# A fourth row buffer, fetches three units ahead, and weight sums spread evenly, in an encoder layer on one core

## The chip, the cores and the metric

The kernel runs on one core of a Trainium2 chip. The metric is the device time of one execution in microseconds (us), lower is better; the median over runs is compared.

## The reference

One layer of a streaming encoder for two groups of tokens, 2048 of a prompt and 8 x 16 of samples, width 1024. Cut to its frame:

```python
h   = rms_norm(x, norm_g[0]);  z = h @ w_in          # 3592 columns
att = band_attention(...)                            # 8 heads x 64, own chunk of 64 and 8 before
mem = mlstm_sequence(...)                            # 4 heads x 128, matrix memory
x   = x + rms_norm(concat(att, mem) @ w_out, norm_g[1])
h   = rms_norm(x, norm_g[2])
u   = h @ w_up                                       # 1024 -> 2 * 2816
y   = b_conv + sum(ext[:, j:j + S] * w_conv[j] for j in range(3))   # causal, depthwise
gate, up = split(y, 2)
ffn = (gelu(gate) * up) @ w_down                     # 2816 -> 1024
x   = x + rms_norm(ffn, norm_g[3])
```

All is float32. The change concerns the last matrix product, `w_down`, alone.

## The kernel before, in words

**Precision.** Every float32 operand `r` of a matrix product is split into a high part (`h`, a cast on ACT, L1259) and the rest (`l = r - h`, on DVE, L1260); `mm3` (L95 to L97) makes three matmuls of each product: high by high, high by low, low by high. So every activation row and every weight block passes a cast and a subtraction before TensorE can use it.

**Stages.** After the projections, attention and memory come 17 token tiles of 128 rows in three blocks (`FBLOCKS`: 6, 6 and 5 tiles). For each block the kernel runs an up stage and then a down stage.

The up stage has 22 units `f` of 128 columns. It computes `u` as a two-by-two block product with seven products in place of eight (P1 to P7), applies the convolution (`conv`: one ACT and two DVE instructions on a row of 768), GELU and the product of the halves, and stores the activation row `g` to DRAM: to `gd` (blocks 0 and 2, called plain), or with six further combinations of the token halves to `gsd` (block 1).

The down stage reads these rows back. In plain blocks it goes twice (`dh` = 0, 1: the two halves of the output's 1024 columns) over 22 steps `k`, one row of `gd` each, with weights in six chunks of four `k` (the last of two); the row is needed again in the second half and fetched again. In block 1 it runs 42 units `q`: seven products (D1 to D7) of six units, each unit a row of `gsd` with two blocks of weights. Four of the seven products need sums or differences of weight quarters. These are made in block 0, beside its down stage, and kept in DRAM (`wtd`).

**Buffers.** Two pools matter. `row` (tag "yq") has three buffers of 128 x 1024 and holds the convolution's rows (`y`, `g`), fetched activation rows (`gr`, `gq`), squares of the norm and evacuated halves. `quad` (tag "q") has eleven buffers of 128 x 512 and holds raw weights (`wu`, `wdr`, `wt`), pieces of the next block's transposed rows, evacuated halves, and the first few activation rows of a down stage, fetched as two halves (`early`), while the convolution still needs the rows. The split parts of an activation row lie in `w3` (four buffers: two rows in flight), those of weights in `wh` and `wl` (two each: the present chunk and the next).

**Fetches.** `fetch(dh, k)` and `fetch_unit(q)` load a row. At the end of the up stage the first ones go early into quads: 0 to 4 in plain blocks, 0 to 3 in block 1. From then on, step k calls the fetch of row k + 2 (L1732, L1733; unit q of q + 2, L1645, L1646). All these DMAs are issued on SP's queue, which takes them one after the other: an instruction there that waits for its data or for a free buffer holds those behind it.

**Sums.** `load_down` (L1324) loads the weights of a chunk. In block 0 every second chunk also loads the other column half of its (up to) two pairs of k into `wt`, and puts four sums a pair, each with its store, into the list `sums`. Each step k calls `step_sums(3)` (L1346), which takes three of them: a DVE operation in place, and its store on SP right behind it.

**Order.** Instructions are written in a program order, but the framework orders each engine's stream itself by a simulated timeline; it also inserts the waits. `tc.keep_in_program_order` ties one instruction behind the one written before it on the same engine, so that it isn't moved ahead of it.

**Beside the down stage** run `ahead` units, one step of them for every k or q: the norm and transposition of the next block's rows (`h2_units`) and the finish of the block before (`later`: loads `f` and `x`, an update on DVE and POOL, the store of the output).

Of the kernel before, what the change touches and what calls it, by code (L numbers as in the profile page):

```python
# [10 lines left out]
F32 = mybir.dt.float32  # L11
F32R = mybir.dt.float32r
AF = mybir.ActivationFunctionType
ALU = mybir.AluOpType
# [3 lines left out]
P = 128  # L18
D = 1024
# [9 lines left out]
NF = 22  # L29
# [15 lines left out]
def hymba_step(ctx: ExitStack, tc: tile.TileContext, I: dict, O: dict):  # L45
    nc = tc.nc
# [69 lines left out]
    wtd = [dt_([P, 2048], f"wtd{i}") for i in range(NF // 2)]  # L116
# [920 lines left out]
    ffn = SimpleNamespace(B=[None] * 7, p4=None)  # L1037
# [11 lines left out]
    def quad(name):  # L1049
        return ffn.p3.tile([P, 512], F32, tag="q", name=name, bufs=11)  # L1050

    def row(name):
        return ffn.p3.tile([P, D], F32, tag="yq", name=name, bufs=3)

    def new_B(i, b):
        pool = ffn.p3 if i < EARLY_B else ffn.p4
# [138 lines left out]
    for n_, (half, gi) in enumerate(seq):  # L1195
        wh, wl, _ = pend
# [5 lines left out]
        i = int(g[2])  # L1202
# [116 lines left out]
    def block_of(src, i, q):  # L1319
        return src[i][:, q * 512:(q + 1) * 512]  # L1320

    sums = deque()

    def load_down(dh, c, keep_sums):  # L1324

        ks = range(4 * c, 4 * c + (4 if c < 5 else 2))
        at = lambda k, h: ((0, 1), (3, 2))[k % 2][h]
        raws_ = []
        w = load_w([block_of(I["w_down"], k // 2, at(k, dh)) for k in ks], f"{dh}_{c}", raws_)
        if keep_sums and c % 2 == dh:  # L1330
            for x, k in enumerate(ks):
                if k % 2:
                    continue
                t = [None] * 4
                for e in range(2):
                    t[at(k + e, dh)] = raws_[x + e]
                    r = t[at(k + e, 1 - dh)] = quad(f"wt{k + e}")
                    nc.sync.dma_start(r, block_of(I["w_down"], k // 2, at(k + e, 1 - dh)))
                for o, x_, y_, op in ((2, 2, 1, ALU.subtract), (1, 1, 0, ALU.subtract), (0, 2, 0, ALU.add),
                                      (3, 3, 0, ALU.subtract)):  # L1340
                    sums.append((t, o, x_, y_, op, wtd[k // 2][:, KEPT_AT[o] * 512:KEPT_AT[o] * 512 + 512]))
        return w

    KEPT_AT = (2, 0, 1, 3)

    def step_sums(count):  # L1346
        for _ in range(min(count, len(sums))):
            t, o, x_, y_, op, dst = sums.popleft()
            nc.vector.tensor_tensor(t[o], t[x_], t[y_], op=op)
            nc.sync.dma_start(dst, t[o])  # L1350

    D1, D6, D2, D7, D5, D4, D3 = range(7)
    W_RAW, W_SUM = 0, 1
# [88 lines left out]
    for b, tiles in enumerate(FBLOCKS):  # L1442
# [100 lines left out]
        for f in range(NF):  # L1543
            w = pend.pop(0)
# [5 lines left out]
            a, d_, ec = ps_mm(f"ua{nm}"), ps_sm(f"ub{nm}"), ps_big(f"uec{nm}")  # L1550
            e, c = ec[:, 0:512], ec[:, 512:1024]
# [10 lines left out]
            w = pend.pop(0)  # L1562
            ahead_of(2 * f + 3)
            if f == NF - 1 and plain:
                split_g(0, 0, w3_tile)
                split_g(0, 1, w3_tile)
                for k in range(2, 5):
                    fetch(0, k, True)
            elif f == NF - 1:
                split_unit(0)  # L1570
                split_unit(1)
                for q in range(2, 4):
                    fetch_unit(q, True)
# [53 lines left out]
        if not plain:  # L1627
# [4 lines left out]
            for q in range(42):  # L1632
# [9 lines left out]
                        pend = [load_up(b + 1, 0, 0, quads[0])]  # L1642
                if q not in parts:
                    split_unit(q)
                if q >= 2:  # L1645
                    fetch_unit(q + 2)  # L1646
                gh, gl = parts.pop(q)
                for k in range(2 if u < 5 else 1):
                    at = u % 2 * 1024 + k * 512
# [33 lines left out]
        for dh in range(2):  # L1683
# [9 lines left out]
            for c in range(6):  # L1693
# [48 lines left out]
            for j in order:  # L1742
# [5 lines left out]
                else:  # L1748
# [7 lines left out]
        step_sums(len(sums))  # L1756
        if not last:
            while ahead.step():
                pass
# [96 lines left out]
```

## Time and profile before

| | before |
|---|---|
| median of 3 runs | 2805.16 us (2804.77 to 2808.17) |
| profiled execution | 2804.53 us, its span 2802.8 us |
| PE busy | 2717.6 us, 97% of the span |
| DVE busy | 1936.8 us, 69% |
| ACT busy | 1422.5 us, 51% |
| POOL busy | 450.3 us, 16% |
| moved by DMA | 516.36 MB, mean 184 GB/s |

Times inside the trace count from the start of the span. PE is TensorE's matmuls, PEld its weight loads, which overlap with them; a busy PE is not a PE at its peak, since matmuls are pipelined. PEclk is the granted share of TensorE's clock. SPq is SP's queue of DMA issues; "<-" in a row of a timeline leads from what is written to what is read, and in brackets to what ended the idle time before the row. L1259 and so on are lines of the kernel; `split` has one pair of lines for weights and activations, so the tile's name tells them apart: `gh`, `gl` are parts of activation rows, `wdh`, `wdl` of the weights.

### The profile page before, as it was taken

How to read it: one execution, taken by the hardware profiler on the slowest of the kernel's cores; microseconds unless marked ns; L12 is line 12 of the kernel's file. 1: busy time of each engine (PE TensorE's matmuls, PEld its weight loads, DVE VectorE, ACT ScalarE, POOL GpSimd, SP SyncE). 2: the span in 40 equal slices, each digit the busy share in tenths (PEclk: the TensorE clock that was granted, in tenths of full speed). 3: DMA queues.
4: the chain of work that ended last, by engine and by line, in shares of the span. 5: the costliest groups of instructions: out<-in, count | busy, mean ns of one | idle time of the engine just before them, and what ended most of it. 6: DMA issues, size and time to landing. Idle time of an engine off the chain costs nothing.

```text
span 2802.8 us, 47259 instructions
## 1 busy us (share of the span) xinstructions
PE 2717.6 (97%) x16488; PEld 2543.9 (91%) x16488; DVE 1936.8 (69%) x3563; ACT 1422.5 (51%) x2872; POOL 450.3 (16%) x876
## 2 busy tenths in 40 slices
PE   8999999999999999999999999999999899999898
PEld 7899999998899998878999987799999688999887
DVE  5344455656456668666989987658888876888755
ACT  4345555544356666543454555445454665555433
POOL 1000010212000003244212210011111221222211
PEclk9999999999999999999999999999999999999999
DMA  5544355557455565356545467855555896555586
GB/s 187 153 125 128 111 173 156 171 158 218 156 159 147 149 182 168 97 191 215 189 164 173 161 218 248 296 171 172 177 168 172 267 322 222 180 170 180 192 283 202
DMA packets 334462, 516.36 MB, mean 184 GB/s; under 512 B 57138, under 2 KB 162830, under 8 KB 334094
## 3 DMA queue, kind: packets, MB, share of 16 engines
q1 hardware_dynamic: 295630, 479.49, 53.3%
q10 hardware_dynamic: 38592, 33.83, 3.6%
q8 instruction: 130, 2.13, 0.3%
q14 instruction: 110, 0.90, 0.1%
HBM read 371.61 MB, written 144.72 MB: 184 GB/s over the span
## 4 chain that ended last, share of the span: by engine, by line
PE 50%; DVE 5%; DMA 4%; issue 1%; ACT 1%; POOL 1%; SPq 0%; DVEq 0%; ACTq 0%; POOLq 0%
PE uec L95 5%; PE uec L96 5%; PE uec L97 5%; PE dn L95 3%; PE dn L97 3%; PE dn L96 3%; PE ua L97 3%; PE ua L95 3%; PE ua L96 3%; PE dnm L95 2%; PE dnm L97 2%; PE wo L95 2%; PE dnm L96 2%; PE wo L97 2%; PE wo L96 2%; PE ub L96 1%
## 5 line engine op out<-in xcount | busy, mean ns | idle before, releaser
L95 PE MATMUL uec<-B,wuh 128*128 128x384 f32 (+1 forms) x720 | 235.7, 328 | 6.4 <-DVE uu L1578 4.9
L96 PE MATMUL uec<-B,wuh 128*128 128x384 f32 (+1 forms) x720 | 235.2, 327 | 0.0
L97 PE MATMUL uec<-B,wul 128*128 128x384 f32 (+1 forms) x720 | 233.5, 327 | 0.0
L1259 ACT CAST wuh<-wu 128x512 fp32r<-128x512 f32 x255 | 141.6, 617 | 96.0 <-PE uec L96 89.9
L95 PE MATMUL dn<-wdh,gh 128*128 128x512 f32 x444 | 176.3, 397 | 6.8 <-ACT gh L1259 4.3
L96 PE MATMUL dn<-wdl,gh 128*128 128x512 f32 x444 | 176.7, 398 | 0.0
L1260 DVE TENSOR_TENSOR wul<-wu,wuh 128x512 fp32r<-128x512 f32 x255 | 164.8, 683 | 3.1 <-DMA x2d<-mx 3.1
L97 PE MATMUL dn<-wdh,gl 128*128 128x512 f32 x444 | 166.5, 400 | 0.0
L395 DVE CUSTOM_DVE_ANT_0 tmp<-s,nb 128x640 f32<-128x640 f32 (+4 forms) x128 | 94.4, 738 | 95.3 <-PE s L385 93.4
L95 PE MATMUL vo<-wi_h,hT 128*128 128x256 f32 x544 | 155.9, 287 | 0.6 <-DVE mt L201 0.6
L97 PE MATMUL vo<-wi_h,hT 128*128 128x256 f32 x544 | 156.3, 287 | 0.0
L96 PE MATMUL vo<-wi_l,hT 128*128 128x256 f32 x544 | 155.5, 286 | 0.0
L95 PEld LDWEIGHTS uec<-B,wuh 128*128 128x128 f32 x720 | 135.0, 188 | 10.0 <-DVE uu L1578 6.8
L95 PE MATMUL qk<-hT,wi_h 128*128 128x384 f32 (+1 forms) x384 | 130.4, 340 | 5.9 <-ACT qk_st L226 5.2
L96 PEld LDWEIGHTS uec<-B,wuh 128*128 128x128 f32 x720 | 135.2, 188 | 0.1
L97 PEld LDWEIGHTS uec<-B,wul 128*128 128x128 f32 x720 | 135.0, 188 | 0.0
L408 DVE TENSOR_TENSOR ptl<-pt,pth 128x640 fp32r<-128x640 f32 (+4 forms) x128 | 93.7, 738 | 57.7 <-ACT pth L407 56.7
L1260 DVE TENSOR_TENSOR gl<-gr,gh 128x768 fp32r<-128x768 f32 (+3 forms) x92 | 75.7, 830 | 82.6 <-ACT gh L1259 82.6
L1259 ACT CAST gh<-gr 128x768 fp32r<-128x768 f32 (+3 forms) x92 | 65.0, 719 | 131.5 <-PE dn L96 100.5
L396 ACT ACTIVATE tmp<-tmp,mn 128x640 f32<-128x640 f32 (+4 forms) x128 | 97.6, 762 | 64.5 <-DVE mn L395 61.8
L1260 DVE TENSOR_TENSOR wdl<-wdr,wdh 128x512 fp32r<-128x512 f32 x165 | 107.8, 696 | 31.8 <-ACT wdh L1259 31.8
L96 PE MATMUL qk<-hT,wi_h 128*128 128x384 f32 (+1 forms) x384 | 129.0, 336 | 0.0
(440 smaller groups left out, 9080.1 us busy)
## 6 DMA issues: line engine op xcount, KB each, us to landing
wu<-in_w_up SPq DMA_DIRECT2D x220, 256.0 KB, 3.9
wu<-wsd SPq DMA_DIRECT2D x176, 256.0 KB, 3.7
wdr<-in_w_down SPq DMA_DIRECT2D x121, 256.0 KB, 5.3
wi_raw<-in_w_in SPq DMA_DIRECT2D x52, 512.0 KB, 4.1
wsd<-ws SPq DMA_DIRECT2D x88, 256.0 KB, 3.2
gr<-gd SPq DMA_DIRECT2D x39, 384.0 KB, 5.7
kraw<-kTd SPq DMA_DIRECT2D x112, 128.0 KB, 3.4
gr<-gd SPq DMA_DIRECT2D x39, 320.0 KB, 4.1
```

Of the source, the lines that this page charges most:

```text
L95: nc.tensor.matmul(out, ah, bh, start=start, stop=False, skip_group_check=onto)
L96: nc.tensor.matmul(out, ah, bl, start=False, stop=False, skip_group_check=onto)
L97: nc.tensor.matmul(out, al, bh, start=False, stop=stop, skip_group_check=onto)
L395: nc.vector.tensor_tensor_reduce(o_, s_, b_, 1.0, 3e38, ALU.add, ALU.min, accum_out=mn)
L396: nc.scalar.activation(tmp[:, :n], tmp[:, :n], AF.Exp, bias=mn, scale=-1.0, accum_out=rsum[:, i % 4, hh:hh + 1])
L408: nc.vector.tensor_tensor(s.ptl[:, sl, qc], ptv, s.pth[:, sl, qc], op=ALU.subtract)
L1259: nc.scalar.copy(h, r)
L1260: nc.vector.tensor_tensor(l, r, h, op=ALU.subtract)
```

## The change

It does four things. The pool `row` gets a fourth buffer. Fetches in the down stages are called for k + 3 and q + 3 in place of k + 2 and q + 2 (in block 1 unit 2 now goes into a row at once instead of two quads). Each chunk of weights of block 0 makes the sums of one pair of k (the eleven pairs are spread over the first eleven of its twelve chunks) in place of up to two pairs in every second chunk. And the sums are timed by a counter of steps: two in the second step after the load was called, two in the third, their stores two steps after each; both are tied to the program order.

```diff
     def row(name):
-        return ffn.p3.tile([P, D], F32, tag="yq", name=name, bufs=3)
+        return ffn.p3.tile([P, D], F32, tag="yq", name=name, bufs=4)
...
-    sums = deque()
+    later_on = []
+    at_step = [0]
...
         w = load_w([block_of(I["w_down"], k // 2, at(k, dh)) for k in ks], f"{dh}_{c}", raws_)
-        if keep_sums and c % 2 == dh:
-            for x, k in enumerate(ks):
-                if k % 2:
-                    continue
-                t = [None] * 4
-                for e in range(2):
-                    t[at(k + e, dh)] = raws_[x + e]
-                    r = t[at(k + e, 1 - dh)] = quad(f"wt{k + e}")
-                    nc.sync.dma_start(r, block_of(I["w_down"], k // 2, at(k + e, 1 - dh)))
-                for o, x_, y_, op in (...):
-                    sums.append((t, o, x_, y_, op, wtd[k // 2][:, ...]))
+        i = 2 * c + (dh if c < 5 else 0)
+        if not keep_sums or (c == 5 and dh):
+            return w
+        t = [None] * 4
+        for k in (2 * i, 2 * i + 1):
+            t[at(k, dh)] = raws_[k - 4 * c]
+            r = t[at(k, 1 - dh)] = quad(f"wt{k}")
+            nc.sync.dma_start(r, block_of(I["w_down"], i, at(k, 1 - dh)))
+
+        def combine(o, x, y, op):
+            tc.keep_in_program_order(nc.vector.tensor_tensor(t[o], t[x], t[y], op=op))
+
+        def store(o, to):
+            tc.keep_in_program_order(nc.sync.dma_start(block_of(wtd, i, to), t[o]))
+
+        for n_, (o, x, y, op, to) in enumerate(...):
+            due = at_step[0] + 2 + n_ // 2
+            later_on.append((due, lambda a=(o, x, y, op): combine(*a)))
+            later_on.append((due + 2, lambda a=(o, to): store(*a)))
         return w
...
-    def step_sums(count):
-        for _ in range(min(count, len(sums))):
-            t, o, x_, y_, op, dst = sums.popleft()
-            nc.vector.tensor_tensor(t[o], t[x_], t[y_], op=op)
-            nc.sync.dma_start(dst, t[o])
+    def step_sums():
+        for x in [x for x in later_on if x[0] <= at_step[0]]:
+            later_on.remove(x)
+            x[1]()
+        at_step[0] += 1
...
-                for q in range(2, 4):
-                    fetch_unit(q, True)
+                fetch_unit(2)
+                fetch_unit(3, True)
...
-                if q >= 2:
-                    fetch_unit(q + 2)
+                if q >= 1:
+                    fetch_unit(q + 3)
...
-                        fetch(dh, k + 2)
+                        fetch(dh, k + 3)
...
-                    if dh == 1 or k >= 3:
-                        fetch(dh + (k + 2) // NF, (k + 2) % NF)
+                    if dh == 1 or k >= 2:
+                        fetch(dh + (k + 3) // NF, (k + 3) % NF)
...
-                    step_sums(3)
+                    step_sums()
```

More of the change, by code (lines that the diff above doesn't have):

```diff
@@ L1329, in load_down @@
         w = load_w([block_of(I["w_down"], k // 2, at(k, dh)) for k in ks], f"{dh}_{c}", raws_)
-        if keep_sums and c % 2 == dh:
-            for x, k in enumerate(ks):
-                if k % 2:
-                    continue
-                t = [None] * 4
-                for e in range(2):
-                    t[at(k + e, dh)] = raws_[x + e]
-                    r = t[at(k + e, 1 - dh)] = quad(f"wt{k + e}")
[L1338 to L1341, printed above, removed]
-        return w
-    KEPT_AT = (2, 0, 1, 3)
-    def step_sums(count):
-        for _ in range(min(count, len(sums))):
-            t, o, x_, y_, op, dst = sums.popleft()
-            nc.vector.tensor_tensor(t[o], t[x_], t[y_], op=op)
-            nc.sync.dma_start(dst, t[o])
+        i = 2 * c + (dh if c < 5 else 0)
[10 more added lines that the diff above has]
+            tc.keep_in_program_order(nc.sync.dma_start(block_of(wtd, i, to), t[o]))
+        for n_, (o, x, y, op, to) in enumerate(((2, 2, 1, ALU.subtract, 1), (1, 1, 0, ALU.subtract, 0),
+                                                (0, 2, 0, ALU.add, 2), (3, 3, 0, ALU.subtract, 3))):
+            due = at_step[0] + 2 + n_ // 2
+            later_on.append((due, lambda a=(o, x, y, op): combine(*a)))
+            later_on.append((due + 2, lambda a=(o, to): store(*a)))
+        return w
+    def step_sums():
[3 more added lines that the diff above has]
+        at_step[0] += 1
     D1, D6, D2, D7, D5, D4, D3 = range(7)
@@ L1755, in hymba_step @@
                     unfinished.append((tiles[j], rs))
-        step_sums(len(sums))
+        while later_on:
+            step_sums()
         if not last:
```

## The prediction

> **What bounds the kernel now.** I first cut the span into its stages by the view of busy time by windows: all before the FFN, then up and down projection of the three token blocks in turn.
>
> ```profile
> core 0: us, PE busy (x) PEld busy (x) DVE busy (x) ACT busy (x) POOL busy (x), PEclk, DMA share, GB/s
> 1322.00:1651.00 329.00, 320.99 (x1824) 316.71 (x1822) 301.58 (x457) 165.97 (x266) 70.45 (x87) 1.00 0.53 178
> 1651.00:1850.00 199.00, 190.02 (x838) 155.04 (x839) 132.67 (x189) 93.91 (x155) 10.87 (x24) 0.98 0.76 257
> 2166.00:2357.00 191.00, 180.59 (x799) 147.11 (x798) 147.60 (x212) 111.59 (x201) 33.76 (x42) 0.96 0.81 275
> 2638.00:2803.00 165.00, 150.93 (x636) 120.93 (x636) 90.58 (x124) 59.85 (x107) 31.86 (x34) 0.97 0.71 243
> ```
>
> The three down stages (lines 2 to 4) have PE idle for 9 to 14 us each and a granted clock under 1.00; elsewhere TensorE hardly stops. TensorE is the bound, and what a change can win is TensorE's gaps. The chain that ended last shows the steady pace: in block 0 the pair "dnm L97 x2" comes back once per step k.
>
> ```profile
> 1779.26 0.47 PE dnm L97 x2
> ...
> 1783.41 0.47 PE dnm L97 x2
> ...
> 1787.55 0.47 PE dnm L97 x2
> ```
>
> So a step is 4.15 us (1783.41 - 1779.26), and with the data there it is TensorE alone. The timeline of PE has the gaps; the bracket is the idle time before the row, and its releaser.
>
> ```profile
> 1652.18 0.50 PE L95 MATMUL dnm<-wdh,gh 128*128 128x512 f32 x1 [1.80 <-ACT wdh L1259]
> ...
> 1667.15 0.50 PE L95 MATMUL dnm<-wdh,gh 128*128 128x512 f32 x1 [1.22 <-ACT gh L1259]
> ...
> 1683.94 0.80 PE L95 MATMUL dnm<-wdh,gh 128*128 128x512 f32 x1 [3.58 <-ACT gh L1259]
> ...
> 1773.00 0.50 PE L95 MATMUL dnm<-wdh,gh 128*128 128x512 f32 x1 [2.28 <-ACT gh L1259]
> ...
> 2200.18 0.80 PE L95 MATMUL dn<-wdh,gh 128*128 128x512 f32 x1 [4.29 <-ACT gh L1259]
> ...
> 2241.23 1.11 PE L1089 MATMUL h2T_pt<-ident,x2r 128*128 128x128 f32 x4 [3.97 <-ACT b L1106]
> ...
> 2652.93 0.50 PE L95 MATMUL dnm<-wdh,gh 128*128 128x512 f32 x1 [1.23 <-ACT gh L1259]
> 2660.27 0.80 PE L95 MATMUL dnm<-wdh,gh 128*128 128x512 f32 x1 [3.35 <-ACT gh L1259]
> ```
>
> Nearly all wait for "gh", the split of an activation row; and nearly all stand in the first steps of a down stage, where the row buffers change hands from the convolution to the fetches. The four longest are followed by slow matmuls (0.80 and 1.11 us long). The windows behind them:
>
> ```profile
> 1683.90:1689.60 5.70, 5.66 (x17) 4.78 (x18) 5.70 (x9) 1.56 (x3) 0.00 (x0) 0.50 0.83 284
> 2200.20:2205.00 4.80, 4.80 (x13) 3.85 (x14) 3.88 (x4) 2.59 (x5) 1.59 (x3) 0.50 0.81 245
> 2241.20:2245.90 4.70, 4.67 (x13) 3.89 (x14) 3.97 (x7) 2.53 (x5) 0.94 (x1) 0.50 0.99 349
> 2660.30:2665.80 5.50, 5.50 (x13) 4.34 (x14) 3.88 (x5) 0.72 (x1) 3.08 (x2) 0.50 1.05 397
> ```
>
> PEclk is 0.50 in all four: half of each window is lost too, 2.85, 2.40, 2.35 and 2.75 us. With its clock the stall at 1684 costs 3.58 + 2.85 = 6.4, that at 2200 6.7, at 2241 6.3, at 2660 6.1 us; the 2.28 us of 1773 cost no clock (its row has the usual 0.50). The Trainium skill's page "TensorE: Matmul & The Clock Gate", section "Part 1: The HAM clock gate (the "warmup" mystery)", says that an idle window of about 3.4 us halves the clock and a busy one of about 3.4 us restores it. By that an estimate for 1684 would be 3.58 + 1.7 = 5.3; the trace has longer cold stretches, and the row decides.
>
> **The change, part by part.** The simulated scheduler of the framework orders each engine, so I price what comes late, not positions.
>
> *Sums, block 0.* The number of operations stays: eleven pairs, each with two extra loads, four subtractions or additions and four stores. Before, two pairs of every second chunk were summed at three a step; now one pair of every chunk, two sums a step, each store two steps behind its sum and tied behind the SP instruction before it. What this is worth is seen on SP, DVE and ACT ahead of the stall of 1684:
>
> ```profile
> 1671.28 1.59 SPq L1338 DMA_DIRECT2D wt<-in_w_down  x2
> 1673.20 0.33 SPq L1590 DMA_DIRECT2D gd<-g  x1
> 1677.97 0.33 SPq L1350 DMA_DIRECT2D wtd<-wt  x1
> 1678.39 0.38 SPq L1503 DMA_DIRECT2D gr<-gd  x1
> ...
> 1677.25 0.69 DVE L1349 TENSOR_TENSOR wt<-wt,wt 128x512 f32<-128x512 f32 x1 [3.31 <-DMA wt<-in_w_down]
> ...
> 1683.05 0.83 ACT L1259 CAST gh<-gr 128x768 fp32r<-128x768 f32 x1 [1.42 <-DMA gr<-gd]
> ```
>
> SP issued nothing from 1673.53 to 1677.97: the store of a sum stood at its head, the sum waited for its second operand, and the fetch of row 5 stood behind the store. It went out at 1678.39, landed at 1683.05, and TensorE waited. With the store two steps (8.3 us) later, and the fetch called one step (4.15 us) earlier, the row lands at about 1673.6 + 4.7 = 1678.3, before step 4 ends (1683.94 - 3.58 = 1680.4). Gain between 0 (another load takes the store's place at SP's head) and 6.4; I take 5.5, since the rows name the store as cause and, with the cast of 0.83 us, the lead is 1680.4 - 1678.3 - 0.8 = 1.3 us.
>
> *The start of block 0.* Eight sums run in the first steps, first and last:
>
> ```profile
> 1644.02 0.69 DVE L1349 TENSOR_TENSOR wt<-wt,wt 128x512 f32<-128x512 f32 x1 [1.85 <-DMA wt<-in_w_down]
> ...
> 1660.43 0.68 DVE L1349 TENSOR_TENSOR wdr<-wdr,wdr 128x512 f32<-128x512 f32 x1
> ...
> 1664.00:1680.00 16.00, 14.78 (x66) 11.69 (x65) 11.80 (x18) 11.11 (x20) 0.96 (x3) 1.00 0.94 326
> ```
>
> That is 8 x 0.68 = 5.4 us of DVE and 1.85 of waiting, while TensorE waits 1.80 and 1.22 us. They leave this place; but the step counter is 0 when both of the first two chunks are loaded, so eight sums fall due in steps 2 and 3. The third row shows DVE with 16 - 11.80 = 4.2 us free there, so at worst 5.4 - 4.2 = 1.2 comes back. Ends: -1.2 to +3.0; I take +1.5, half the gaps, because the convolution of the last unit holds DVE there as well.
>
> *What the sums add.* A pair now holds four of the eleven quarter-row buffers ("q") from its load to its landed stores, some six steps instead of about three, so the next chunk finds seven for its six loads, and the pieces of the next block's transposed rows want the same buffers. The second half of the stage shows no gap at all with the old bursts, so I cost it at nothing; what it costs without that cover is the second rival. Tying adds no wait of its own: what is queued behind a tied store on SP is the next fetch, and its row is needed three steps on.
>
> *Fourth row buffer and three units ahead, block 1.* In the old trace the first fetch into a row buffer (unit 4), and the split that it holds up, are
>
> ```profile
> 2195.48 1.03 SPq L1527 DMA_DIRECT2D gq<-gsd  x2
> ...
> 2199.30 0.83 ACT L1259 CAST gh<-gq 128x768 fp32r<-128x768 f32 x1
> ...
> 2206.00:2246.00 40.00, 34.68 (x152) 27.54 (x151) 34.62 (x46) 23.77 (x42) 11.43 (x10) 0.91 0.92 320
> ```
>
> It waited for the convolution's last row product and landed under TensorE's gap. Now unit 2 takes a row early and frees it when it is split, and unit 4 can go then, a step or more earlier. That removes up to 6.7 us at 2200. But just behind it, 2206 to 2246 (third row), the DMA engines are busy 0.92 of the time, and the stall of 2241 stands there, where no row is the releaser. Reaching that stretch 6.7 us earlier asks the same bytes of it in less time. So I take half, 3.3; ends 0 and 6.7 + 6.3 = 13.0. The fetch of unit 2 in one transfer instead of two saves one issue on SP, which has gaps: nothing.
>
> *Block 2.* Here the first row fetch stands behind the store of the last activation:
>
> ```profile
> 2648.48 0.32 SPq L1590 DMA_DIRECT2D gd<-g  x1
> 2648.85 0.42 SPq L1503 DMA_DIRECT2D gr<-gd  x1
> ...
> 2658.41 0.62 ACT L1259 CAST wdh<-wdr 128x512 fp32r<-128x512 f32 x1 [0.23 <-DMA wdr<-in_w_down]
> 2659.49 0.72 ACT L1259 CAST gh<-gr 128x640 fp32r<-128x640 f32 x1 [0.47 <-DMA gr<-gd]
> ```
>
> A fourth buffer lets it go before that product is made. The 1.23 us at 2652.93 should go; at 2660 the split also stood behind weight casts on ACT that waited for their own transfer, so of 6.1 I take 1.8. Sum 3.0; ends 0 and 7.3.
>
> *Up stages and the stage before the FFN.* The convolution's rows get the fourth buffer too. The first row of the stage windows has DVE at 301.58 of 329 us, and no DVE work goes away: nothing, ends -3 and +3.
>
> Sum: 5.5 + 1.5 + 3.3 + 3.0 = 13.3 us. The profiled execution took 2804.53 us around a span of 2802.8, 0.6 under the median of 2805.16. So 2804.5 - 13.3 = 2791.2, and on the scale of the medians 2792.
>
> **The rivals.**
> 1. *The transfers are the limit, or the fetch is held by something else.* For it: DMA share 0.94 at 1664 to 1680 and 0.92 at 2206 to 2246, and other waits stand on SP. Then each stall moves a few steps on. Against it: 397 GB/s in the last clock window, so 320 is no ceiling. The page "DMA: Bandwidth & Descriptors" of the Trainium skill, section "Specifications", gives about 358 GB/s of HBM per core; the 397 here is above that. Gains remain below 3 us: 2803.
> 2. *The other side: weight loads starve for quarter-row buffers.* Place: the edges between chunks in block 0 and the change of halves near 1773, where the four held buffers, the six loads and two evacuated halves come together, twelve on eleven. A late weight chunk costs a wait like 1684's, 6.4 us. There are eleven edges. The 6.3 us of blocks 1 and 2 stay; it gets slower than before from the first late edge if block 0 gains nothing, measurably (over 5.6 us) from the second: 2 x 6.4 - 6.3 = +6.5; with three late, +12.9 and 2818. Against it: a chunk is needed four steps, 16.6 us, after its load is called, and the page's section on DMA issues has its landing at 5.3.
>
> ```profile
> wdr<-in_w_down SPq DMA_DIRECT2D x121, 256.0 KB, 5.3
> ```
>
> 3. *Everything goes:* 6.4 + 3.0 + 2.3 + 13.0 + 7.3 = 32.0, the whole of the quoted gaps; with 27 of it the time is 2778. For it: an earlier fetch helps every start alike.
>
> **How the numbers follow.** Forecast 0.65 (its own range 2781 to 2801), rival 1 0.16, rival 2 0.09, rival 3 0.10. A difference under 0.2% (5.6 us) is about what a measurement of this kernel can't tell from none. Of the forecast 0.03 lies inside that band, so faster is 0.62 + 0.10 = 0.72, same 0.19, slower 0.09. The range 2778 to 2808 takes in rival 1 and leaves half of rival 3 and rival 2 out, some 0.15.
>
> **What would show it.** Right: in block 0 a row fetch goes out on SP between 1670 and 1675 and the gap of 3.58 with its half clock is gone; no sum on DVE before the third step; stores never head SP with an unfinished sum; the gap of 4.29 in block 1 is under 1.5, the 1.23 in block 2 gone; the down stages' PEclk nearer 1.00. Wrong: new gaps with "wdh" as releaser at chunk edges of block 0 (rival 2), or the same gaps a few steps on with DMA releasers (rival 1). The forecast fails most easily in block 1, if the gap at 2241 grows by what 2200 loses.

## The result, and the profile after

The changed kernel takes 2790.07 us (median of six runs, 2784.68 to 2792.67) against 2804.89 us (2800.39 to 2808.17): a ratio of 0.9948, 95% interval 0.9935 to 0.9961, 14.8 us faster. Its profiled execution took 2789.77 us, the span 2787.7.

The view of busy time by windows, with the borders at the first and last matmul of each down projection; first the kernel before (three down stages):

```profile
core 0: us, PE busy (x) PEld busy (x) DVE busy (x) ACT busy (x) POOL busy (x), PEclk, DMA share, GB/s
1652.20:1855.80 203.60, 195.80 (x863) 159.74 (x864) 135.66 (x194) 94.73 (x157) 10.25 (x22) 0.98 0.76 256
2177.00:2360.10 183.10, 173.40 (x755) 139.72 (x754) 139.25 (x198) 106.77 (x193) 32.29 (x39) 0.96 0.83 281
2630.00:2794.80 164.80, 158.10 (x674) 127.17 (x672) 92.56 (x130) 61.42 (x107) 29.76 (x31) 0.98 0.71 243
```

and the changed kernel, its first up stage ahead of them:

```profile
1326.00:1652.00 326.00, 320.15 (x1824) 316.85 (x1823) 302.93 (x459) 166.84 (x266) 64.33 (x88) 1.00 0.53 179
1653.50:1848.00 194.50, 192.49 (x863) 157.63 (x864) 136.26 (x195) 93.49 (x157) 17.16 (x21) 1.00 0.81 270
2169.20:2352.50 183.30, 172.65 (x755) 136.98 (x754) 139.50 (x197) 106.54 (x192) 35.73 (x39) 0.99 0.83 279
2619.70:2779.80 160.10, 157.71 (x685) 128.51 (x684) 97.29 (x136) 64.26 (x112) 32.18 (x33) 0.99 0.73 255
```

The number after each pair of borders is the stage's length. Blocks 0 and 2 are some 9 and 4.6 us shorter, PE idles 2.0 and 2.4 us there in place of 7.8 and 6.7. Block 1 is as long as it was: its clock rose from 0.96 to 0.99, and PE idles 10.7 us in place of 9.7. What TensorE waited for is in PE's timeline of the changed kernel:

```profile
1756.91 0.48 PE L95 MATMUL dnm<-wdh,gh 128*128 128x512 f32 x1 [1.36 <-DVE fr L1387]
...
2191.15 0.79 PE L95 MATMUL dn<-wdh,gh 128*128 128x512 f32 x1 [3.04 <-ACT gh L1259]
...
2202.04 0.50 PE L97 MATMUL dnm<-wdh,gl 128*128 128x512 f32 x1 [1.15 <-DVE gl L1260]
...
2212.17 0.50 PE L95 MATMUL dnm<-wdh,gh 128*128 128x512 f32 x1 [1.56 <-ACT gh L1259]
...
2259.48 0.48 PE L1089 MATMUL h2T_pt<-ident,x2r 64*128 64x64 f32 x8 [1.46 <-DVE x2r L1081]
...
2631.00 0.64 PE L95 MATMUL dn<-wdh,gh 128*128 128x512 f32 x1 [2.10 <-DVE ug L1466]
```

In block 0 the gaps of 3.58 and 2.28 us are gone and one of 1.36, behind the evacuation of a half ("fr"), is new; in block 2 those of 1.23 and 3.35 are gone. In block 1 the 4.29 us became 3.04, the 3.97 at 2241 vanished, and a string of 1 to 1.6 us stands in its place. The new gap in block 0 stands at the change of halves, and DVE's timeline has what leads to it: DVE works without a break from 1748.3 us on, with a sum ahead of the evacuation that TensorE waits for.

```profile
1754.28 0.68 DVE L1341 TENSOR_TENSOR wdr<-wdr,wdr 128x512 f32<-128x512 f32 x1
...
1756.08 1.28 DVE L1387 COPY fr<-dnm 128x512 f32<-128x512 f32 x2
```

SP's timeline in block 0 answers to the one of before:

```profile
1668.64 0.38 SPq L1510 DMA_DIRECT2D gr<-gd  x1
...
1671.78 1.62 SPq L1510 DMA_DIRECT2D gr<-gd  x2
1673.45 1.12 SPq L1344 DMA_DIRECT2D wtd<-wt  x2
```

The first fetch into a row goes out at 1668.64 (1678.39 before), two more at 1671.78, and the first stores of sums behind them, when their sums are done. Over the whole stage a store still waits for its sum on SP six times, 4.1 us in all, where it was 24 times and 25.5 us.

One table for all that follows: stage lengths in us of one profiled execution each, from the first to the last down-projection matmul of a block (`down`), and from there to the next (`up`). `pre` ends with the first up-projection matmul; the change does not reach into it, yet it lies between 1317.0 and 1326.8 us over these executions. So totals differ by some us for no reason of the change, and the stages tell more than the totals. The stages have a spread of their own: with the same instructions in the same order on every engine, block 0 took 194.6 and 196.9 us (changed and q2), block 2 159.9 to 161.2 us (changed, q2, x2r_tied, store_at_once, no_finish). An edit elsewhere can also change the order that the framework gives a stage: store_at_once edits block 0 alone, and its block 1 took 181.3 us in place of 183.4. The last column has, for block 1, the time in which PE idles and the granted clock, by the view by windows.

| kernel | median us | ratio to before [95%] | pre | up 0 | down 0 | down 1 | up 2 | down 2 | idle us, PEclk of down 1 |
|---|---|---|---|---|---|---|---|---|---|
| before | 2804.89 | | 1321.8 | 330.4 | 203.7 | 183.2 | 269.9 | 164.7 | 9.7, 0.96 |
| changed | 2790.07 | 0.9948 [0.9935, 0.9961] | 1326.7 | 326.8 | 194.6 | 183.4 | 267.1 | 160.1 | 10.7, 0.99 |
| row4 | 2793.36 | 0.9962 [0.9949, 0.9975] | 1324.4 | 329.6 | 203.8 | 175.9 | 267.1 | 166.0 | 4.7, 0.98 |
| fetch3 | 2795.08 | 0.9971 [0.9961, 0.9982] | 1324.9 | 331.7 | 199.1 | 186.0 | 267.1 | 162.0 | 13.5, 0.99 |
| sums_only | 2796.40 | 0.9969 [0.9957, 0.9981] | 1326.1 | 331.3 | 194.7 | 182.9 | 269.9 | 164.0 | 9.0, 0.97 |
| sums_row4 | 2784.60 | 0.9937 [0.9925, 0.9950] | 1324.1 | 325.2 | 194.8 | 176.3 | 267.1 | 165.4 | 4.6, 0.98 |
| q2 | 2779.73 | 0.9909 [0.9894, 0.9924] | 1322.0 | 325.6 | 196.9 | 176.1 | 267.1 | 161.2 | 4.9, 0.99 |
| x2r_tied | 2786.47 | 0.9944 [0.9931, 0.9956] | 1319.6 | 327.4 | 196.3 | 184.5 | 267.1 | 159.9 | 10.5, 0.98 |
| cast_first_x | 2782.76 | 0.9927 [0.9910, 0.9944] | 1322.2 | 325.4 | 198.7 | 178.5 | 267.1 | 162.5 | 7.3, 0.99 |
| cast_first_q2x | 2790.10 | 0.9943 [0.9926, 0.9961] | 1326.8 | 325.9 | 196.5 | 181.2 | 267.1 | 161.2 | 9.2, 0.99 |
| store_at_once | 2788.19 | 0.9942 [0.9925, 0.9958] | 1323.7 | 326.3 | 197.4 | 181.3 | 267.1 | 160.4 | 7.3, 0.98 |
| no_finish | 2779.24 | 0.9916 [0.9901, 0.9932] | 1317.0 | 326.7 | 194.9 | 177.8 | 267.1 | 159.9 | 6.0, 0.99 |
| out_on_pool | 2784.46 | 0.9933 [0.9920, 0.9947] | 1322.1 | 325.5 | 194.9 | 184.3 | 267.1 | 161.1 | 8.7, 0.97 |
| fetch_tied_pool | 2782.84 | 0.9918 [0.9898, 0.9937] | 1322.1 | 325.3 | 195.8 | 180.0 | 267.1 | 161.2 | 8.2, 0.99 |

The up stage of block 1 is 321.1 us in all of them. Each kernel has its own runs of before beside it (medians 2802.15 to 2806.04), so kernels are compared by their ratios.

### The profile page after: what moved, and what is told of

Read it like the earlier page. It is cut to its first block, busy times and chain, and to the rows that moved or that the text cites. A ratio compares the mean times of both kernels' runs of the same rounds, so it can differ in the third digit from the quotient of the medians.

```text
span 2787.7 us, 47226 instructions
## 1 busy us (share of the span) xinstructions
PE 2711.9 (97%) x16488; PEld 2539.5 (91%) x16488; DVE 1939.6 (70%) x3562; ACT 1421.7 (51%) x2871; POOL 447.3 (16%) x876
## 4 chain that ended last, share of the span: by engine, by line
PE 51%; DVE 4%; DMA 3%; issue 1%; POOL 1%; ACT 1%; SPq 0%; DVEq 0%; POOLq 0%; ACTq 0%
PE uec L95 6%; PE uec L97 6%; PE uec L96 6%; PE dn L97 3%; PE dn L95 3%; PE dn L96 3%; PE ua L97 3%; PE ua L96 3%; PE ua L95 3%; PE dnm L97 2%; PE dnm L95 2%; PE dnm L96 2%; PE wo L95 2%; PE wo L96 2%; PE wo L97 2%; PE ub L96 1%
## 5 line engine op out<-in xcount | busy, mean ns | idle before, releaser
L97 PE MATMUL qk<-hT,wi_l 128*128 128x384 f32 (+1 forms) x384 | 128.6, 335 | 0.0
L96 PE MATMUL qb<-hT,wi_h 128*128 128x384 f32 (+1 forms) x384 | 127.8, 333 | 0.0
```

What stands on the lines that cost most here:

```text
L96: nc.tensor.matmul(out, ah, bl, start=False, stop=False, skip_group_check=onto)
L97: nc.tensor.matmul(out, al, bh, start=False, stop=stop, skip_group_check=onto)
```

## The experiments

### The parts one by one

**row4**, the kernel before with the fourth row buffer alone, and **fetch3**, the same with all fetches three ahead:

```diff
-        return ffn.p3.tile([P, D], F32, tag="yq", name=name, bufs=3)
+        return ffn.p3.tile([P, D], F32, tag="yq", name=name, bufs=4)
```

> The kernel before with a fourth row buffer alone (fetches two ahead, old sums). Theory: the buffer frees the convolution, so the gain of the up stages (3.6 us in block 0, 2.8 in block 2 by the two traces) comes from it alone, and the down stages keep their gaps of 3.58 and 4.29 us, since the store of a sum and the last row product still hold the fetch: about 2799 us. Rival (the buffer does nothing without the longer lead): 2805, every stage as before.

> The kernel before with the fourth row buffer and the fetches three ahead, but with the old sums. Theory (a store at SP's head holds the fetch in block 0): block 0 keeps a gap of 2 to 4 us with half clock near its fifth step, block 2 loses its two gaps; 2804.9 - 6.4 (up stages) - 4.6 (down stage of block 2) = about 2794. Rival (the lead of three units alone is enough, the sums don't matter): block 0's down stage falls to some 195 us as well, 2786 to 2790.

**sums_only**, the kernel before with the new sums alone (the changed kernel with `bufs=3` and every fetch at `+ 2`):

> The kernel before with the new sums alone (three row buffers, fetches two ahead). Theory: the gap of 3.58 us in block 0 with its half clock and the 1.80 and 1.22 us at its start go, so the down stage of block 0 falls from 203.7 us to some 195, and blocks 1 and 2 stay as before: 2804.9 - 9 = about 2796. Rival (the late row comes from the buffers, not from the sums): block 0 stays at 203 us, 2805. If the held quarter-row buffers starve the weights, it is slower than before.

Measured: the new sums alone make the whole gain of block 0's down stage (203.7 to 194.7 us, with all in place 194.6), as expected. The fourth buffer does nothing there (203.8). Its own gains are elsewhere: 2.8 us in the third up stage (269.9 to 267.1, the same in each kernel that has it), and 7.3 us in block 1 (183.2 to 175.9). So row4's 2793.36 lies under both times expected: the gap of 4.29 us stays (4.08), but the one of 3.97 at 2241 is gone. Three ahead gives block 2 another 4.0 us (166.0 to 162.0), block 0 with the old sums 4.7 (203.8 to 199.1; PE's idle time falls by 2.2 us, the rest is mostly granted clock, 0.98 to 1.00), and takes 10.1 from block 1 (175.9 to 186.0). fetch3's 2795.08 is near its 2794, but not by the gaps that were foreseen: block 0 keeps one of 1.49 us without half clock, and block 2 still has 3.06 and 1.45. Here is block 1 of row4, the whole stage and the stretch behind its first gap, from the view by windows:

```profile
2178.90:2354.80 175.90, 171.18 (x755) 138.22 (x755) 138.59 (x198) 106.24 (x193) 37.98 (x39) 0.98 0.86 294
...
2206.00:2256.00 50.00, 50.00 (x230) 41.00 (x229) 47.28 (x66) 34.83 (x62) 20.44 (x14) 0.99 0.97 351
```

PE is busy in all of these 50 us while the transfers move 351 GB/s. The changed kernel in the like stretch, 26 us into its stage:

```profile
2195.00:2245.00 50.00, 44.15 (x198) 33.83 (x197) 39.10 (x52) 30.07 (x51) 15.22 (x13) 1.00 0.87 298
```

It idles 5.9 us and moves less, 298 GB/s. So a ceiling of the transfers' rate isn't what holds it.

### Where the stores stand

**store_at_once**, each store right behind its sum:

```diff
-            later_on.append((due + 2, lambda a=(o, to): store(*a)))
+            later_on.append((due, lambda a=(o, to): store(*a)))
```

> The changed kernel with the store of each weight sum written right behind its sum, not two steps later. Theory (a store that waits on SP for its sum holds the row fetch queued behind it): gaps of over 1.5 us come back in the down stage of the first block, which grows from 194.6 us to 198 to 204 us; time 2793 to 2799 us. Rival (the gain came from one pair of rows per chunk in place of two in every other chunk, and the place of the stores costs nothing): the stage stays at 194 to 196 us, time 2789 to 2791 us.

Measured: 197.4 us, 0.6 under the theory's range and 2.8 over the changed kernel. The same instructions differ by nearly as much: block 0 of q2 below has the changed kernel's one for one and took 196.9. One gap of over 1.5 us did come back, 1.98 us at the change of halves; there ACT's cast of the row stands behind weight casts that wait for late loads, and SP's waits for a sum from 1742 to 1766 us come to 0.4 us, so it is not the theory's wait. The median, 2788.19, is a little under the rival's times. The view of waits of SP's queue in the down stage of block 0 says why the stores cost so little; before:

```profile
SPq L1350 <- DVE wt L1349: 14.7, 14, 3.8
SPq L1350 <- DVE wdr L1349: 10.8, 10, 5.3
```

(total us, times, longest), and store_at_once:

```profile
SPq L1344 <- DVE wdr L1341: 5.1, 14, 1.2
...
SPq L1344 <- DVE wt L1341: 1.9, 8, 0.3
```

The stores' 25.5 us of waiting for sums shrank to 7.0 with the store directly behind the sum as before (4.1 with the two steps between). The sum now falls due two steps after its load and mostly finds its operand landed: DVE idles 1.4 us, once, for one here, where it was 9.6 us in three times before. So the stores' two steps of grace are worth nothing that these runs can tell; the gain lies in the sums' two steps, in the even spread or in both, which no run here separates.

### Block 1: the load ahead of the fetch (a theory that fell)

In the changed kernel the fetch of unit 4 leaves SP at 2185.09, behind a load of x2 that had waited. **x2r_tied** ties that load to its written place:

```diff
-                    nc.sync.dma_start(rows_[t], x2d[t])
+                    ld = nc.sync.dma_start(rows_[t], x2d[t]); late or tc.keep_in_program_order(ld)
```

> The changed kernel with one more tie: in the down stages the load of the next block's rows (x2r) stays behind the fetches written before it. Theory: in block 1 the fetch of unit 4 went out late (2185.09) because that load stood before it on SP and waited for a buffer of the convolution; tied, the fetch goes out some 4 us earlier, the gap of 3.04 us with its half clock (1.7) is gone, and the time is about 2790 - 4.7 = 2785. Rival (the transfers are the limit in block 1): the gap comes back within the next ten units, the down stage of block 1 stays at 183 us and the time at 2790.

Measured: the fetch leaves 11.7 us into the stage in place of 15.9, 7.3 us before TensorE falls idle, and the gap is the same. The timelines of SP, of ACT and of PE in x2r_tied:

```profile
2176.10 0.42 SPq L1534 DMA_DIRECT2D gq<-gsd  x1
...
2183.47 2.18 ACT L1259 CAST wdh<-wdr 128x512 fp32r<-128x512 f32 x4 [2.38 <-PE dnm L97]
2185.56 0.83 ACT L1259 CAST gh<-gq 128x768 fp32r<-128x768 f32 x1
...
2186.44 0.50 PE L95 MATMUL dn<-wdh,gh 128*128 128x512 f32 x1 [3.04 <-ACT gh L1259]
```

The cast of unit 4 ("gh") stands on ACT behind four casts of weights ("wdh"), and those wait until TensorE has done with the weight buffer that they write. TensorE then has nothing to do until 2.18 us of casts and the 0.83 us of its own row are over: 3.04 us. The Trainium skill's page "Perfetto Trace Analysis", section "Tensor Engine Instruction (MATMUL, LD_WEIGHTS)", says that ACT's queue is strictly first in, first out; the trace agrees, the landed row passes none of the four. The kernel before had the same order, in a row that the prediction did not show (ACT's timeline of before):

```profile
2195.97 2.18 ACT L1259 CAST wdh<-wdr 128x512 fp32r<-128x512 f32 x4 [2.73 <-PE dnm L97]
2198.06 1.05 ACT L1077 ACTIVATE sq<-x2r 128x1024 f32<-128x1024 f32 x1
...
2199.30 0.83 ACT L1259 CAST gh<-gq 128x768 fp32r<-128x768 f32 x1
```

There a square of the norm ("sq") stands ahead of the row as well, and the late fetch fits too: it left at 2195.48, and the same fetch took 4.0 us to land in row4, which would be 2199.5, so the row can hardly have been there before its cast. But in row4 it left 2.6 us earlier in the stage and landed at 2198.84, and 4.08 us of the gap stayed, with the casts and the square still ahead. In the changed kernel the square stands behind the row's cast, and 3.04 us are left.

### Block 1: the cast ahead of the casts

**cast_first_x** is x2r_tied with the split written before the next weights, and the casts of the fourth block's weights tied behind it:

```diff
+                if q not in parts:
+                    split_unit(q)
                 if u % 2 == 0:
                     wh, wl = pend
                     if q < 40:
                         pend = load_block(b, q // 2 + 1)
...
-                if q not in parts:
-                    split_unit(q)
```

```diff
-    def split(h, l, r):
-        nc.scalar.copy(h, r)
-        nc.vector.tensor_tensor(l, r, h, op=ALU.subtract)
+    def split(h, l, r, tie=False):
+        i = nc.scalar.copy(h, r)
+        k = nc.vector.tensor_tensor(l, r, h, op=ALU.subtract)
+        if tie:
+            tc.keep_in_program_order(i)
...
-            split(h_[:, cc], l_[:, cc], raw)
+            split(h_[:, cc], l_[:, cc], raw, tie)
...
-        return load_w([...], f"{b}_{q}")
+        return load_w([...], f"{b}_{q}",
+                      None, q == 3)
```

> The changed kernel with the load of x2 rows tied in its written place, and in the middle block the cast of unit 4 ahead of the four weight casts of the block after next on ScalarE. Theory (ScalarE's order holds unit 4): the gap of 3.04 us some 19 us into the stage goes, with some 1.7 us of half clock behind it; the stage falls from 184.5 us (with the tied load alone) to 179 to 181 us and the time from 2786.5 us to 2781 to 2783 us. Rival (the stage is set by the weights of the fifth block, which come late whatever happens before): the gap goes, those 20 to 70 us later grow from some 7 us to some 11 us, and the time stays at 2785 to 2788 us.

Measured: 178.5 us, 6.0 less than x2r_tied, at 2782.76. ACT's timeline of cast_first_x:

```profile
2184.80 0.83 ACT L1259 CAST gh<-gq 128x768 fp32r<-128x768 f32 x1 [0.70 <-DMA gq<-gsd]
2186.48 2.18 ACT L1259 CAST wdh<-wdr 128x512 fp32r<-128x512 f32 x4 [0.85 <-PE dnm L97]
```

The gap of 3.04 us is gone, and the half clock right behind it (1.28 us is left at 2188.59, for the other part, "gl"). With the row fetched early, ACT's order was the cause of that gap; the order alone, without the tied load, was not tried. The idle time behind it comes to 7.5 us in x2r_tied and 6.1 here, so the rival, by which it grows, falls.

### Block 1: two ahead there alone

**q2** is the changed kernel with the fetches of block 1 as they were:

```diff
-                fetch_unit(2)
-                fetch_unit(3, True)
+                for q in range(2, 4):
+                    fetch_unit(q, True)
...
-                if q >= 1:
-                    fetch_unit(q + 3)
+                if q >= 2:
+                    fetch_unit(q + 2)
```

> The changed kernel with the fetches of the middle block alone two units ahead again; the other two blocks stay at three ahead, the fourth buffer and the new sums stay. Theory (reaching three ahead costs the middle block what the fourth buffer gained it): the down stage of the middle block falls from 183.4 us to 175 to 178 us, as in the kernel of before with the fourth buffer alone (175.9), the other stages stay, and the time is 2781 to 2784 us. Rival (the new sums or the buffer's other users, not the reach, set the middle block): it stays at 182 to 185 us and the time at 2789 to 2792 us.

Measured: 176.1 us and 2779.73, both as the theory has them. By its ratio it is the fastest of all here: 0.9909 [0.9894, 0.9924] of before, an interval that lies wholly below the changed kernel's. By the view by windows, its block 1:

```profile
2165.60:2341.70 176.10, 171.17 (x756) 137.45 (x755) 139.98 (x198) 106.30 (x192) 37.67 (x39) 0.99 0.86 293
```

**sums_row4** has two ahead everywhere:

> The changed kernel with every fetch two units ahead: fourth buffer and new sums only. Theory (parts add): first down stage 194 to 197 us, middle 175 to 177 us, last 165 to 167 us, the third up stage 267.1 us; time 2782 to 2786 us, so some 5 us faster than the changed kernel and 4 to 5 us slower than it with only its middle block at two ahead (2779.7 us). Rival (three ahead is needed in the first block as well): the first stage is over 199 us and the time over 2787 us.

Measured: 194.8, 176.3, 165.4 and 267.1 us, 2784.60: the parts add up. Three ahead is worth 4 to 5 us in block 2, nothing in block 0 once the sums are spread, and costs 7 us in block 1.

**cast_first_q2x** puts both cures of block 1 together:

> Both edits: the middle block fetched two ahead, its cast of unit 4 first, the load of x2 rows tied. If the two losses are independent, the stage of the middle block falls to 169 to 172 us and the time to 2772 to 2777 us; if they share one cause (the weights' transfers), it stays near 176 us and the time near 2780 us.

Measured: neither. The gap of 4.08 us that q2 keeps there falls to 0.92, but gaps of 1 to 2 us appear 47 to 113 us into the stage, and it takes 181.2 us, 5 more than q2. The cures are not independent. The engines' order further on differs from q2's; which instruction there is at fault, no run here tells.

### Block 1: what the reach costs

The changed kernel and q2 differ on SP in where the loads of the fifth weight block stand. SP's timeline of the changed kernel:

```profile
2199.62 3.88 SPq L1424 DMA_DIRECT2D out_y_prompt<-f  x2
2203.62 0.36 SPq L1534 DMA_DIRECT2D gq<-gsd  x1
2204.02 2.05 SPq L1313 DMA_DIRECT2D wdr<-wtd  x4
```

and of q2:

```profile
2192.13 3.21 SPq L1313 DMA_DIRECT2D wdr<-wtd  x4
2195.76 3.08 SPq L1424 DMA_DIRECT2D out_y_prompt<-f  x2
```

Counted from the stages' starts (2169.16 and 2165.64) the loads go at 34.9 and 26.5 us. In ACT's timeline of the changed kernel the casts wait for them, with the casts of rows queued behind:

```profile
2209.20 0.62 ACT L1259 CAST wdh<-wdr 128x512 fp32r<-128x512 f32 x1 [6.77 <-DMA wdr<-wtd]
```

Two things stand ahead of them on SP in the changed kernel: stores of finished rows, which wait for GpSimd, and a row fetch three units ahead. **no_finish** leaves out the finishing of block 0's rows in block 1 (those rows are not written):

```diff
-        done = [u for t, rs in unfinished for u in later(t, rs)]
+        done = [u for t, rs in unfinished for u in later(t, rs)] if b != 1 else []
```

> The changed kernel without the finishing of the first block's six output tiles in the middle block (36 transfers of 256 KB, their scaling and their sum are left out; those output rows are not written). The third block finishes its rows as before. Theory (in the middle block the weights come late because they share SP's queue and the transfers with the finishing rows): of the seven gaps 30 to 90 us into the stage (7 us in all) under 2 us are left, the gap of 3.04 us stays (it hangs on ScalarE's order), and the stage falls from 183.4 us to 174 to 178 us; time 2780 to 2785 us. Rival (fetching three ahead itself delays the weights, with or without these rows): the stage stays over 181 us and the time over 2787 us.

**out_on_pool** keeps them, but stores from GpSimd's queue:

```diff
-            nc.sync.dma_start(out_rows(t)[:, c:c + 512], v)
+            nc.gpsimd.dma_start(out_rows(t)[:, c:c + 512], v)
```

> The changed kernel with the finished rows of the first and middle blocks stored from GpSimd's queue in place of SP's. The bytes stay; only SP no longer waits for GpSimd (17.7 us in ten waits in the 105 us from 2185 us on). Theory (SP's wait for the finished row holds the weight loads behind it): the middle block's stage falls from 183.4 us to 177 to 180 us, time 2783 to 2787 us. Rival (the transfers themselves limit it): the stage stays at 182 to 186 us, time 2789 to 2793 us. A loss is possible if the issue on GpSimd costs that engine time or if its transfers are dearer.

Measured: without the finishing, 177.8 us and 2779.24, the time a little under the one expected; the 3.04 us gap stays, and of the smaller ones between 30 and 90 us into the stage 2.3 us are left where under 2 were expected. Together with the stores it takes out loads, sums and transfers (235 GB/s in the stage, 279 in the changed kernel), so it can't tell which of them cost the time. With the stores on the other queue the stage, 184.3 us, is the rival's, but the time, 2784.46, is the theory's. Both belong together: PE idles 8.7 us in place of 10.7, and in this execution the clock (0.97 for 0.99) takes back more than that. So the wait for GpSimd may cost some 2 us; one execution doesn't settle it. The fetch took over part of its place. SP's timelines, out_on_pool

```profile
2189.98 7.10 SPq L1534 DMA_DIRECT2D gq<-gsd  x2
2197.13 1.85 SPq L1313 DMA_DIRECT2D wdr<-wtd  x4
```

and no_finish:

```profile
2183.17 6.81 SPq L1534 DMA_DIRECT2D gq<-gsd  x4
2190.03 1.85 SPq L1313 DMA_DIRECT2D wdr<-wtd  x4
```

In both the row fetches occupy SP's head for some 7 us, and the weights go out behind them, 33.5 and 30.4 us into the stage. In the two 70-us stretches from 2190 on, the waits of SP for the subtraction that frees a row buffer come to 15.2 and 25.0 us:

```profile
SPq L1534 <- DVE gl L1260: 15.2, 6, 6.3
```

```profile
SPq L1534 <- DVE gl L1260: 25.0, 8, 6.4
```

**fetch_tied_pool** adds to out_on_pool that the fetch of every second unit stands behind the weight loads written before it:

```diff
-                nc.sync.dma_start(g[q], src)
+                ld = nc.sync.dma_start(g[q], src)
+                if q >= 4 and q % 2:
+                    tc.keep_in_program_order(ld)
```

> The kernel with the finished rows stored from GpSimd's queue, and in the middle block every second row fetch (from unit 5 on) tied behind the weight loads written ahead of it; still three units ahead, the same transfers. Theory (a row fetch three ahead stands on SP before a buffer is free, 7.1 us for two of them, with the weight loads of the fifth block behind it): those four loads are issued 25 to 28 us into the stage in place of 33.5, and the middle block's stage falls from 184.3 us to 175 to 179 us; time 2776 to 2780 us. Rival (the transfers of the rows three ahead slow the weights wherever they stand on SP): the loads are issued earlier but the stage stays over 181.5 us, time 2782 to 2786 us.

Measured: the loads go 26.3 us into the stage, as early as in q2. The stage falls by 4.3 us to 180.0, between the two ranges, and the time, 2782.84, is the rival's. The view by windows of block 1, out_on_pool and then fetch_tied_pool:

```profile
2163.70:2348.00 184.30, 175.57 (x756) 138.75 (x755) 140.38 (x197) 106.91 (x192) 42.51 (x51) 0.97 0.82 278
2164.40:2344.40 180.00, 171.79 (x756) 136.70 (x755) 139.96 (x197) 107.46 (x192) 45.59 (x51) 0.99 0.82 284
```

PE's idle time falls by half a microsecond only, from 8.73 to 8.21; most of the 4.3 us is granted clock. Part of that can't come from the edit: the gap of 3.04 us, 22 us into the stage in both, is followed by a clock of 0.50 in one and 0.67 in the other over 3.4 us. In q2, with its loads just as early, PE idles 4.9 us. So late loads of the fifth block are not what the reach costs, or not alone. SP's timeline and, for 2196 to 2207 us, its waits:

```profile
2190.68 2.64 SPq L1313 DMA_DIRECT2D wdr<-wtd  x4
2193.70 3.59 SPq L1534 DMA_DIRECT2D gq<-gsd  x2
```

```profile
SPq L1069 <- PE h2T_pt L1089: 6.5, 1, 6.5
```

Another blocker has come forward: a load of x2 stands on SP for 6.5 us until TensorE has transposed the rows in its buffer, and the loads of the sixth weight block follow it. That it keeps the idle time up fits the trace but wasn't tried by itself. What is shown is that the reach costs block 1 some 7 us (q2, sums_row4); by which wait, these runs leave open.

## Why the prediction was right in its sum, and where its steps were not

The forecast was 2792 and 2790.07 was measured. Against the profiled execution of before, down 0 and up 0 gave 9.1 and 3.6 us, down 1 lost 0.2, up 2 and down 2 gave 2.8 and 4.6: 19.9, less 4.9 by which the unchanged part ahead of the FFN ran longer, is 15.0 of the 15.1 us between the spans. The forecast sum was 13.3, so that the two totals agree is in part luck: the stages that the change reaches gave 19.9 us, and 4.9 were lost where it doesn't reach. Of the terms, that of block 1 failed; those of block 0, of block 2 and of the up stages were too low and made up for it.

- *Sums, block 0 (5.5) and the start of block 0 (1.5).* Right in mechanism, low in size: 9.1 and 3.6. The 2.28 us at 1773 went too, which the sum had not priced. sums_only shows that the sums alone make the 9.1, and the first row fetch leaves SP at 1668.64, a little ahead of the span forecast (1670 to 1675). The first sum runs at 1668.1, not before the third step, as foretold. One step of the reasoning is not borne out: the two steps by which a store follows its sum. store_at_once drops them and keeps 6.3 of the 9.1 us, where the same instructions differ by 2.3; and a store did still head SP with an unfinished sum, for 4.1 us in all. The start pays only where the sums and the fourth buffer come together: up 0 is 329.6 and 331.3 us with one of them, 325.2 with both.
- *What the sums add (0).* Held for the weights: no gap at a chunk's edge in block 0 has them as releaser, and rival 2 did not occur. But the term is not nothing: at the change of halves, the place that rival 2 names, the sums stand on DVE ahead of the evacuation, and TensorE waits 1.36 us for it. A gap of 1.0 to 2.6 us with that releaser is in nine of the eleven kernels with the new sums and in none of the three without.
- *Fourth buffer and three ahead, block 1 (3.3).* This step failed: -0.2. It took the late fetch for the cause of the gap at 2200. In row4 the fetch leaves 2.6 us earlier in the stage than before and 4.08 of the 4.29 us stay; x2r_tied sends it 4.3 us earlier than the changed kernel and keeps its 3.04; cast_first_x changes ACT's order as well and loses them. And it priced two edits as one: the buffer alone gives 7.3 us (row4), and three ahead takes that back (sums_row4 176.3, changed 183.4, q2 176.1). The working looked at what is queued behind a waiting instruction on SP only for the tied stores, not for a row fetch that waits for its buffer (7.1 us for two in out_on_pool). Whether that wait is what takes the gain back stays open: with the weights put ahead of it PE still idled 8.2 us. The place was foreseen (just behind the gap), its cause not: it is no lack of transfer rate, since row4 moves 351 GB/s there, the changed kernel 298.
- *Block 2 (3.0).* 4.6, within its ends of 0 and 7.3. The 1.23 us gap is gone, and the 3.35 too; one of 2.10 us, 11 us into the stage and behind the convolution's input, is left.
- *Up stages (0, -3 to +3).* The third one gained 2.8 us in every kernel with four buffers: at the end of that range and mis-sized at nothing. Only DVE's busy time was weighed, not the wait for a row buffer; that this wait is what went, no run here shows by itself.
- *The rivals.* Rival 1 (gains below 3 us) did not come, nor did rival 3 (32 us). q2, at 2779.73, comes near rival 3's 2778, but not by all quoted gaps going: the one at 2200 is still 4.08 us there, and up 2 gave 2.8 us that rival 3 does not count.

## What to carry to other kernels

A buffer and a longer reach are two edits: give the buffer first, then try the reach stage by stage, since a fetch issued before its buffer is free stands at the head of its queue and holds whatever is behind it (7.1 us for two fetches in out_on_pool). When a gap's releaser is a cast or a copy, read that engine's rows ahead of it before blaming the transfer: here the row had landed, and four other casts stood in front. And read idle time and granted clock apart before a stage's gain is put down to an edit: here 4.3 us of stage held half a microsecond of idle time, and 2 us less idling hid behind a lost clock.

## What the runs showed of the hardware

How long a gap is does not settle whether TensorE loses its clock; where it falls does. PE's timeline of q2 has one of 1.80 us and one of 2.76 us:

```profile
1751.84 0.47 PE L95 MATMUL dnm<-wdh,gh 128*128 128x512 f32 x1 [1.80 <-DVE fr L1387]
...
2620.89 0.47 PE L95 MATMUL dn<-wdh,gh 128*128 128x512 f32 x1 [2.76 <-DVE ug L1466]
```

In each of the fourteen traces the half-clock stretches of the stages from the first up projection to the last down projection last 3.41 us, or two times that in a row, and begin on one grid of 3.41 us. The view by windows along q2's grid (PE's busy time is the second number, PEclk the third from the end):

```profile
1749.00:1752.40 3.40, 1.60 (x8) 1.01 (x7) 3.40 (x7) 1.87 (x4) 0.00 (x0) 1.00 0.60 199
1752.40:1755.80 3.40, 3.40 (x10) 2.63 (x9) 3.40 (x6) 3.34 (x11) 0.73 (x3) 0.50 0.91 315
...
2616.00:2619.40 3.40, 2.13 (x14) 1.82 (x12) 2.46 (x5) 1.38 (x3) 0.00 (x0) 1.00 0.03 11
2619.40:2622.80 3.40, 1.91 (x8) 1.59 (x9) 3.40 (x8) 2.74 (x7) 0.71 (x2) 1.00 0.44 163
2622.80:2626.20 3.40, 3.32 (x15) 2.42 (x14) 3.40 (x7) 0.42 (x2) 0.94 (x1) 1.00 0.39 122
```

The shorter gap lies in one window: PE idles 1.80 of its 3.40 us, and the next window runs at half clock, which costs 1.7 us. The longer one is shared by two, 1.27 and 1.49 us, and costs nothing. Laid over all fourteen traces, each of the 33 windows at full clock in which PE idled for 1.89 us or more was followed by half clock; of those with 1.75 us or less, one was (x2r_tied, 1.38 us), and why is open; between the two both occur.

The Trainium skill's page "TensorE: Matmul & The Clock Gate", section "Part 1: The HAM clock gate (the "warmup" mystery)", says that the window that the gate watches runs freely, so that the point of the change depends on where work falls in it; that agrees with the grid and with a gap whose price varies. Its rule that an idle window of about 3.4 us is needed does not: here 1.80 us of idle time in a window sufficed. This is also what separates two executions of the same instructions: in block 0 the changed kernel has a gap of 1.36 us and a clock of 1.00 over the stage, q2 one of 1.80 us and the 1.7 us of lost clock, which is 2.1 of the 2.3 us between the stages.
